# Output projection's last block by token tile for six of its eight steps, and four smaller edits at the border to the ConvFFN

## The chip, the cores and the metric

One Trainium2 chip, one of its cores. The metric is the device time of one execution in microseconds (us); the kernel before ran three times, with a median of 2329.59 us.

TensorE (PE in the profile) multiplies, VectorE (DVE) and ScalarE (ACT) work on tiles in on-chip memory and read the accumulators of TensorE, GpSimd (POOL) does what is left to it, and SyncE (SP) issues nearly all DMAs.

## The reference, cut to what matters

One layer of a diffusion backbone on 256 latent tokens of width 2048, float32. Four token mixers (a convolution, two linear-attention scans, an RWKV scan) run side by side on a normalised input; their outputs are gated, summed and projected. The change lies where that projection ends and the ConvFFN begins:

```
mx = merge_branches(...)          # sum of gated branches, then  @ w_out  (2048 x 2048)
x  = x + gt1x * rms_norm(mx, g1)
fx = conv_ffn(modulate(rms_norm(x, g2), sh2x, sc2x), ffn_up, ffn_dw, ffn_down)
x  = x + gt2x * rms_norm(fx, g3)
```

`rms_norm` is over the 2048 channels of a token, so the norm of x needs every output column of `@ w_out` for that token. `sh2x`, `sc2x`, `gt1x` and `gt2x` are slices of the adaLN product `silu(c) @ w_mod + b_mod` with w_mod 2048 x 12288.

## The kernel before, in words

**Precision and weights.** Each product is made of three matmuls on numbers split into a high and a low part: hi x hi, hi x lo, lo x hi. `load_split` (L187) brings 256 rows by 512 columns of a weight (512 KB) into a tile `raw` by a DMA on SP (L194), copies it to `hi` on ScalarE (L198) and subtracts `hi` from `raw` into `lo` (L200). The subtraction is on VectorE, but for as many calls as the counter `pool_lo` says it is on GpSimd; the counter is 0 at first and is set to 3 at L1468, ahead of the first FFN weights. `hi` and `lo` come from rings of buffers.

**The output projection** (`out_proj`, L1382). The 256 tokens are two token tiles of 128, the 2048 output columns four blocks `db` of 512. For a block, `mode_a` (L226) takes the 2048 inner rows in eight steps `kg`; a step has 6 matmuls of 128x512 for each token tile, so 96 in a block. Usually a step does both token tiles. With `apart=3`, as in the last block, the last three steps are held back and then run token tile by token tile: tile 0 for the three steps, then tile 1. The odd steps of that block use a ring of their own (`hlp`, two buffers).

After a block, for each token tile, ScalarE sums the squares of the result (L1411) and VectorE multiplies it by a gain into `mg` (L1412). After the last block `residual(i)` (L1395) follows for both tiles, one after the other, written behind the evacuation of both: the mean and a reciprocal root of the squares (`mean_rsqrt` L1373, with the seven short VectorE instructions of `rsqrt`, L104 to L115; `an`), four 512-column pieces of x + rs * mg on VectorE (L1400), their squares on ScalarE (L1402), and again mean and root (`ff`).

**The start of the FFN** (`ffn`, L1424). The second root goes on the diagonal of a matrix (`ffdiag`, L1437). `transpose_split` (L1352) multiplies x by it, for each of 16 column tiles kt, into an accumulator tile `psts` that holds both token tiles of the column; ScalarE applies shift and scale (`tst`, L1369), VectorE copies the high part (`u2h`, L1370) and subtracts it for the low part (`u2l`, L1371). Then `mode_b` (L207) runs `ffn_up` against u2: 11 pairs of blocks of eight steps, results in `psB`. Two accumulator tiles (`aux`) serve `psts` and the adaLN products.

**The adaLN product** is fed in between as a generator of steps (`mod_feed`, L296; `wmod_steps`, L248). A step loads 512 KB of w_mod (L260) and does eight matmuls into `psw`; eight steps make a block, which ends in a copy (L268), four matmuls `psf`, an addition on VectorE (L278) and a product on GpSimd (L279). `feed` (L305) takes steps until a fractional counter is reached. Ahead of the transposes L1443 takes 8 steps (`96 + 8`), after that 0.25 step for each step of `mode_b`. In the FFN `wmr` is None (L1618), so these loads use the five `raw` buffers of the FFN weights.

**What sets the order.** Each engine runs its queue in order. The queues are written before the run by the framework's planner (the kernel turns on its timeline simulation), which places instructions by their simulated readiness and, among the ready ones, in the order of the source. SP's queue is planned in the same way. A buffer that comes to lie on memory of an earlier pool waits tile by tile (`reuse_waits`) until the earlier tile has been used for the last time.

Of the kernel before, what the change touches and what calls it, by code (L numbers as in the profile page):

```python
# [11 lines left out]
F32 = mybir.dt.float32  # L12
# [8 lines left out]
P = 128  # L21
# [20 lines left out]
class Kern:  # L42
# [144 lines left out]
    def load_split(self, parts, width, rings=None):  # L187

        nc = self.nc
        raw = self.raw()  # L190
        hip, lop = rings or (self.hip, self.lop)
        for ap, o in parts:
            w = ap.shape[1]
            nc.sync.dma_start(out=raw[:, :, o : o + w], in_=ap.rearrange("(k p) c -> p k c", p=P))  # L194
        hi = hip.tile([P, 2, 512], F32R, tag="hi", name="hi")
        lo = lop.tile([P, 2, 512], F32R, tag="lo", name="lo")
        s = (slice(None), slice(None), slice(0, width))
        nc.scalar.activation(hi[s], raw[s], AF.Copy)  # L198
        self.pool_lo -= 1
        (nc.gpsimd if self.pool_lo >= 0 else nc.vector).tensor_tensor(lo[s], raw[s], hi[s].bitcast(F32), ALU.subtract)  # L200
        return hi, lo
# [24 lines left out]
    def mode_a(self, parts_of, uh, ul, nkt, toks, evac, apart=0, rings=None):  # L226

        ps = [self.mmp.tile([P, 512], F32, tag="mm", name="psA") for _ in toks]
        n2 = nkt // 2
        held = []  # L230
        for kg in range(n2):
            hl = self.load_split(parts_of(kg), 512, rings if kg % 2 else None)
            todo = [(kg, hl, ti) for ti in range(len(toks))]
            if kg >= n2 - apart:
                held.append(todo)
                todo = [t[ti] for ti in range(len(toks)) for t in held] if kg == n2 - 1 else []
            for g, (hi, lo), ti in todo:
                t0 = toks[ti]
                for k in range(2):
                    kt = 2 * g + k  # L240
                    for j, (u, w) in enumerate(((uh, hi), (uh, lo), (ul, hi))):
                        self.mm(ps[ti], u[:, kt, t0 : t0 + P], w[:, k, :],
                                start=(kt == 0 and j == 0), stop=(kt == nkt - 1 and j == 2))
            self.feed()
        evac(ps)


    def wmod_steps(self, cb, dst, raws=None, gain=None):  # L248
# [8 lines left out]
        for j in range(8):  # L257
            wr = raws or self.wmr
            raw = self.raw() if wr is None else wr.tile([P, 2, 512], F32, tag="wraw", name="wraw")
            nc.sync.dma_start(out=raw, in_=w[256 * j : 256 * j + 256, 512 * cb : 512 * cb + 512].rearrange("(k p) c -> p k c", p=P))  # L260
# [1091 lines left out]
    def transpose_split(self, src, c0, hi_of, lo_of, diag=None, mod=None):  # L1352
# [3 lines left out]
        for kt in range(KT):  # L1356
# [10 lines left out]
            else:  # L1367
                t = self.resp.tile([P, 256], F32, tag="tst", name="tst", bufs=3)
                nc.scalar.activation(t, ps[:, 0:256], AF.Identity, bias=mod[1][:, kt : kt + 1], scale=mod[0][:, kt : kt + 1])  # L1369
                nc.vector.tensor_copy(hi_of(kt), t)  # L1370
                nc.vector.tensor_tensor(lo_of(kt), t, hi_of(kt).bitcast(F32), ALU.subtract)  # L1371
# [10 lines left out]
    def out_proj(self):  # L1382
# [8 lines left out]
        wo = A["w_out"][0]  # L1391
        rings = self.hlp, self.hlp
        self.rs2 = []
# [11 lines left out]
        for db in range(4):  # L1405
            cs = slice(512 * db, 512 * db + 512)

            def ev(pss):
                for i, ps in enumerate(pss):
                    jk = self.resp.tile([P, 512], F32, tag="junk", name="junk", bufs=2)  # L1410
                    nc.scalar.activation(jk, ps, AF.Square, accum_out=ss[:, i, db : db + 1])  # L1411
                    nc.vector.tensor_tensor(mg[:, i, cs], ps, G1[:, cs], ALU.mult)  # L1412
                if db == 3:
                    residual(0)
                    residual(1)

            self.mode_a(lambda kg: [(wo[256 * kg : 256 * kg + 256, cs], 0)], self.uh, self.ul, KT, [256, 384], ev,
                        *((3, rings) if db == 3 else ()))
            if db < 2:
# [4 lines left out]
    def ffn(self):  # L1424
# [15 lines left out]
        self.fs = self.pool("ffs", bufs=2)  # L1440
        self.wap, self.rate, self.modmax = None, 0.25, 128
        self.G[1] = fp.tile([P, D], F32, name="G2")
        self.feed(96 + 8)  # L1443
        self.fed = float(self.modn)
# [22 lines left out]

        self.pool_lo = 3  # L1468
        for s in range(11):
# [75 lines left out]
    def build(self):  # L1545
# [27 lines left out]
        self.fed, self.rate, self.modn, self.modmax = 0.0, 0.0, 0, 96  # L1573
        self.pool_lo = 0
        self.mod2, self.G = self.cp.tile([P, 32, 1], F32, name="mod2"), [None, None]
# [30 lines left out]
        self.dbg("yl", self.ul[:, :, 0:256].bitcast(F32))  # L1606
        self.mgw = self.pool("mgw", bufs=3, stack=ues)
        self.mgp = self.pool("mgp", stack=ues)
        self.mg = self.mgp.tile([P, 2, D], F32, name="mg")
        self.hlp = self.pool("hlp", bufs=2, stack=ues)  # L1610
        self.resp = self.pool("resp", side="right")
# [3 lines left out]
        for i, n in enumerate((3, 0, 2, 1)):  # L1615
            self.merge(i == 0, n)
        self.out_proj()
        self.wmr = None  # L1618
        ues.close()
# [7 lines left out]
        self.hip = self.pool("hip2", bufs=4)  # L1627
        self.lop = self.pool("lop2", bufs=4)
        self.mmes = mes
        self.ffn()  # L1630
# [55 lines left out]
```

## Time and profile before

| | |
|---|---|
| three runs, us | 2334.24, 2325.4, 2329.59 (median 2329.59) |
| profiled execution, us | 2329.05 |
| its span, us | 2327.1 |
| TensorE busy | 2215.9 us, 95% of the span |
| VectorE busy | 1449.6 us, 62% |
| ScalarE busy | 989.5 us, 43% |
| GpSimd busy | 507.6 us, 22% |
| granted TensorE clock, mean | 0.977 |

A line of a timeline view gives the start, the duration, the engine, the line of the code, the operation with its output and inputs, the number of instructions, and in brackets how long the engine was idle before and what ended that. The chain view follows the work that ended last back through what released it. In a table of windows each stretch has its length, then the busy time of each engine (number of instructions), the granted TensorE clock, the DMA share and the GB/s. Times within the trace count from the start of the span.

### The profile page before, as it was taken

Reading aid. Unit: us, or ns where it says so; the run is one execution under the profiler, and the core shown is the slowest. Engines: PE = TensorE matmul, PEld = TensorE weight load, DVE = VectorE, ACT = ScalarE, POOL = GpSimd, SP = SyncE. Lnnn points to the kernel's source line nnn. Section 1 sums busy time; section 2 is a strip of 40 time slices with the busy share of each in tenths; the row PEclk is TensorE's granted clock in tenths of the full one; section 3 lists DMA queues with packets and bytes.
Section 4 is the critical chain, followed back from the end, with each engine's and each line's share of the span. In section 5 each row is a group of like instructions: output and inputs, shape, how many; then the busy total and the mean of one; then the engine's idle time right before and its main releaser. Section 6 shows DMA issues by size and latency. Waiting matters only on the chain.

```text
span 2327.1 us, 42867 instructions
## 1 busy us (share of the span) xinstructions
PE 2215.9 (95%) x16828; PEld 1812.0 (78%) x16828; DVE 1449.6 (62%) x3027; ACT 989.5 (43%) x1493; POOL 507.6 (22%) x865
## 2 busy tenths in 40 slices
PE   6979889999999989999999899989999999999998
PEld 3657667877888666777777678779999999998886
DVE  3357766734555678457565476577776677775554
ACT  4225644533554344334236434444443444444443
POOL 0012553533454599210010033010000000000000
PEclk8989999999999999999999999989999999999999
DMA  9934663555666776787777476567677666666663
GB/s 369 352 115 127 170 183 113 159 171 170 199 188 180 231 208 209 231 247 237 226 231 256 139 257 217 181 231 222 212 222 217 202 182 183 179 205 202 194 193 101
DMA packets 273867, 471.97 MB, mean 203 GB/s; under 512 B 41761, under 2 KB 80929, under 8 KB 272673
## 3 DMA queue, kind: packets, MB, share of 16 engines
q1 hardware_dynamic: 273378, 467.14, 64.8%
q8 instruction: 132, 2.16, 0.4%
q10 hardware_dynamic: 288, 2.10, 0.2%
q14 instruction: 69, 0.57, 0.1%
HBM read 440.33 MB, written 28.84 MB: 202 GB/s over the span
## 4 chain that ended last, share of the span: by engine, by line
PE 78%; DVE 8%; DMA 7%; POOL 4%; ACT 2%; issue 2%; SPq 0%; DVEq 0%; ACTq 0%; POOLq 0%
PE psB L79 37%; PE psA L79 18%; PE psD L79 10%; PE psw L79 4%; DMA wraw<-in_w_mod 3%; DVE lo L200 2%; POOL ctap L874 1%; DMA raw<-in_w_mix 1%; PE psG L79 1%; POOL cacc L875 1%; ACT hi L198 1%; PE psn L79 1%; DMA raw<-in_w_in 1%; PE psf L79 1%; DVE cacc L869 1%
## 5 line engine op out<-in xcount | busy, mean ns | idle before, releaser
L200 DVE TENSOR_TENSOR lo<-raw,hi 128x1024 fp32r<-128x1024 f32 (+2 forms) x485 | 599.2, 1236 | 458.7 <-ACT hi L198 450.0
L198 ACT ACTIVATE hi<-raw 128x1024 fp32r<-128x1024 f32 (+2 forms) x488 | 509.2, 1045 | 796.5 <-PE psB L79 348.6
L79 PE MATMUL psB<-u2h,hi 128*128 128x256 f32 x1408 | 399.5, 286 | 1.2 <-DVE u2h L1370 1.2
L79 PE MATMUL psB<-u2l,hi 128*128 128x256 f32 x1408 | 398.8, 284 | 0.5 <-DVE u2l L1371 0.5
L79 PE MATMUL psB<-u2h,lo 128*128 128x256 f32 x1408 | 399.0, 284 | 0.0
L79 PE MATMUL psA<-lo,uh 128*128 128x512 f32 x832 | 337.4, 406 | 18.4 <-DVE lo L200 18.0
L79 PE MATMUL psA<-hi,ul 128*128 128x512 f32 x832 | 332.7, 400 | 0.0
L79 PE MATMUL psA<-hi,uh 128*128 128x512 f32 x832 | 311.4, 405 | 3.2 <-DVE mg L1344 2.1
L79 PE MATMUL psB<-uh,hi 128*128 128x256 f32 (+1 forms) x832 | 281.0, 346 | 18.7 <-ACT hi L198 16.4
L79 PE MATMUL psB<-ul,hi 128*128 128x256 f32 (+2 forms) x832 | 278.5, 339 | 0.0
L79 PEld LDWEIGHTS psB<-u2h,hi 128*128 128x128 f32 x1408 | 269.6, 192 | 10.9 <-issue 9.5
L79 PEld LDWEIGHTS psB<-u2l,hi 128*128 128x128 f32 x1408 | 270.5, 192 | 0.7 <-DVE u2l L1371 0.7
L79 PE MATMUL psB<-uh,lo 128*128 128x256 f32 (+2 forms) x832 | 263.0, 339 | 8.1 <-DVE lo L200 8.1
L79 PEld LDWEIGHTS psB<-u2h,lo 128*128 128x128 f32 x1408 | 270.5, 192 | 0.1
L79 PEld LDWEIGHTS psA<-lo,uh 128*128 128x128 f32 x832 | 158.1, 190 | 68.5 <-DVE lo L200 27.5
L79 PEld LDWEIGHTS psB<-uh,hi 128*128 128x128 f32 x832 | 158.6, 191 | 51.2 <-ACT hi L198 18.5
L79 PEld LDWEIGHTS psA<-hi,uh 128*128 128x128 f32 x832 | 154.7, 190 | 53.2 <-issue 12.2
L79 PEld LDWEIGHTS psA<-hi,ul 128*128 128x128 f32 x832 | 158.3, 190 | 36.5 <-issue 2.6
L79 PEld LDWEIGHTS psB<-uh,lo 128*128 128x128 f32 (+1 forms) x832 | 152.8, 189 | 32.0 <-DVE lo L200 10.5
L79 PEld LDWEIGHTS psB<-ul,hi 128*128 128x128 f32 (+1 forms) x832 | 157.8, 190 | 23.1 <-issue 6.4
L1541 DVE TENSOR_TENSOR lo<-raw,hi 128x1024 fp32r<-128x1024 f32 x88 | 107.7, 1226 | 78.5 <-ACT hi L1540 78.5
L1461 DVE SCALAR_TENSOR_TENSOR facc<-fpad,ffdw,facc 128x256 f32<-128x256 f32 x352 | 152.8, 490 | 0.2
(573 smaller groups left out, 3028.8 us busy)
## 6 DMA issues: line engine op xcount, KB each, us to landing
raw<-in_w_in SPq DMA_DIRECT2D x208, 512.0 KB, 4.3
raw<-in_ffn_up SPq DMA_DIRECT2D x176, 512.0 KB, 3.8
wraw<-in_w_mod SPq DMA_DIRECT2D x160, 512.0 KB, 5.1
raw<-in_ffn_down SPq DMA_DIRECT2D x88, 512.0 KB, 4.5
raw<-in_w_br SPq DMA_DIRECT2D x32, 512.0 KB, 5.1
raw<-in_w_out SPq DMA_DIRECT2D x32, 512.0 KB, 4.4
raw<-in_w_mod SPq DMA_DIRECT2D x32, 512.0 KB, 3.8
raw<-in_w_in SPq DMA_DIRECT2D x48, 256.0 KB, 4.1
```

The costliest lines, as they stand in the source:

```text
L79: self.nc.tensor.matmul(out, lhsT, rhs, start=start, stop=stop)
L198: nc.scalar.activation(hi[s], raw[s], AF.Copy)
L200: (nc.gpsimd if self.pool_lo >= 0 else nc.vector).tensor_tensor(lo[s], raw[s], hi[s].bitcast(F32), ALU.subtract)
L869: nc.vector.scalar_tensor_tensor(a, cpad[:, i, t : t + 256], w(i, t), a, ALU.mult, ALU.add)
L874: nc.gpsimd.tensor_scalar(m, cpad[:, i, t : t + 256], w(i, t), None, ALU.mult)
L875: nc.gpsimd.tensor_tensor(a, a, m, ALU.add)
L1461: nc.vector.scalar_tensor_tensor(s3(acc), pad[:, dy : dy + 4, dx : dx + 64], tap(t, b), s3(acc), ALU.mult, ALU.add)
L1541: nc.vector.tensor_tensor(f(lo), f(raw), f(hi).bitcast(F32), ALU.subtract)
```

## The change

- `mode_a` of the last block holds back six steps of eight (`apart=6`), and the steps 4 to 7 use the rings of their own; these are now two pools, one for `hi` and one for `lo`, with four buffers each, opened after the merge's buffers are closed.
- `residual(i)` is called for each token tile behind that tile's own evacuation.
- GpSimd subtracts no weights any more: `pool_lo` is gone, the first three FFN weights are subtracted on VectorE like the others.
- The high part of u2 is copied by ScalarE instead of VectorE.
- The adaLN steps in the FFN load into two buffers of their own (`wmr2`); five steps instead of eight are taken ahead of the transposes, then 0.3 for each step of `mode_b`; the gain tile `G2` moves to a pool of its own.

```diff
 load_split:
         nc.scalar.activation(hi[s], raw[s], AF.Copy)
-        self.pool_lo -= 1
-        (nc.gpsimd if self.pool_lo >= 0 else nc.vector).tensor_tensor(lo[s], raw[s], hi[s].bitcast(F32), ALU.subtract)
+        nc.vector.tensor_tensor(lo[s], raw[s], hi[s].bitcast(F32), ALU.subtract)
 mode_a:
-            hl = self.load_split(parts_of(kg), 512, rings if kg % 2 else None)
+            hl = self.load_split(parts_of(kg), 512, rings if kg >= n2 - apart + 2 else None)
 wmod_steps:
-            raw = self.raw() if wr is None else wr.tile([P, 2, 512], F32, tag="wraw", name="wraw")
+            raw = wr.tile([P, 2, 512], F32, tag="wraw", name="wraw")
 transpose_split:
-                nc.vector.tensor_copy(hi_of(kt), t)
+                nc.scalar.activation(hi_of(kt), t, AF.Copy)
 out_proj:
-        rings = self.hlp, self.hlp
+        rings = self.hlp
...
-                if db == 3:
-                    residual(0)
-                    residual(1)
+                    if db == 3:
+                        residual(i)
...
-                        *((3, rings) if db == 3 else ()))
+                        *((6, rings) if db == 3 else ()))
 ffn:
-        self.wap, self.rate, self.modmax = None, 0.25, 128
-        self.G[1] = fp.tile([P, D], F32, name="G2")
-        self.feed(96 + 8)
+        self.wap, self.rate, self.modmax = None, 0.3, 128
+        self.G[1] = self.pool("ffg").tile([P, D], F32, name="G2")
+        self.feed(96 + 5)
...
-        self.pool_lo = 3
 build:
-        self.mgw = self.pool("mgw", bufs=3, stack=ues)
         self.mgp = self.pool("mgp", stack=ues)
         self.mg = self.mgp.tile([P, 2, D], F32, name="mg")
-        self.hlp = self.pool("hlp", bufs=2, stack=ues)
+        mws = ExitStack()
+        self.mgw = self.pool("mgw", bufs=3, stack=mws)
...
+        mws.close()
+        self.hlp = self.pool("hip1", bufs=4, stack=ues), self.pool("lop1", bufs=4, stack=ues)
         self.out_proj()
-        self.wmr = None
...
+        self.wmr = self.pool("wmr2", bufs=2)
```

More of the change, by code (lines that the diff above doesn't have):

```diff
@@ L1573, in build @@
         self.fed, self.rate, self.modn, self.modmax = 0.0, 0.0, 0, 96
-        self.pool_lo = 0
         self.mod2, self.G = self.cp.tile([P, 32, 1], F32, name="mod2"), [None, None]
```

## The prediction

> **What bounds the kernel now.** I read the page first, then the FFN in windows, then the chain and each engine's timeline across the border between output projection and FFN.
>
> ```profile
> 1520.00:1530.00 10.00, 5.48 (x64) 1.67 (x60) 8.87 (x37) 6.28 (x19) 1.17 (x3) 0.73 0.87 311
> 1530.00:1540.00 10.00, 7.56 (x31) 6.62 (x32) 8.73 (x17) 6.08 (x9) 7.24 (x4) 0.59 0.69 234
> 1540.00:1550.00 10.00, 8.85 (x62) 8.64 (x61) 8.01 (x16) 3.68 (x6) 1.25 (x1) 0.83 0.57 173
> 1550.00:1565.00 15.00, 15.00 (x129) 14.90 (x127) 10.88 (x21) 8.87 (x13) 0.00 (x0) 1.00 0.51 148
> ```
>
> From 1550 on TensorE is busy without a gap (15.00 of 15.00). In the thirty microseconds before it is idle for 8.1 (4.52 + 2.44 + 1.15), at a granted clock of 0.73 to 0.83. All that the change touches lies just ahead of or in this hole, so only the hole can give time; what it had absorbed, and no longer does, goes onto TensorE's path.
>
> The hole begins where the last output-projection matmul ends, T = 1495.17 + 24.78 = 1519.95 in the chain, and ends when the second column of u2 has its high part, at 1541.40 (T+21.45):
>
> ```profile
> 1495.17 24.78 PE psA L79 x106
> ```
>
> ```profile
> 1517.75 0.69 DVE L1412 TENSOR_TENSOR mg<-psA,G 128x512 f32<-128x512 f32 x1 [6.56 <-ACT junk L1411]
> ...
> 1520.07 0.16 DVE L114 TENSOR_TENSOR an0ra<-an0ra,an 128x1 f32<-128x1 f32 x1
> 1520.77 0.69 DVE L1412 TENSOR_TENSOR mg<-psA,G 128x512 f32<-128x512 f32 x1 [0.54 <-ACT junk L1411]
> ...
> 1521.63 2.74 DVE L1400 SCALAR_TENSOR_TENSOR x<-mg,an0ry,x 128x512 f32<-128x512 f32 x4
> ...
> 1526.25 1.41 DVE L1400 SCALAR_TENSOR_TENSOR x<-mg,an1ry,x 128x512 f32<-128x512 f32 x2
> 1527.58 0.15 DVE L111 SCALAR_TENSOR_TENSOR ff0ra<-ff0ra 128x1 f32<-128x1 f32 x1
> 1527.65 1.41 DVE L1400 SCALAR_TENSOR_TENSOR x<-mg,an1ry,x 128x512 f32<-128x512 f32 x2
> ...
> 1529.90 0.16 DVE L1378 TENSOR_REDUCE ff<-ss 128x1 f32<-128x4 f32 x1 [0.18 <-ACT junk L1402]
> ...
> 1531.31 2.21 DVE L112 SCALAR_TENSOR_TENSOR ff1ry<-ff1ra,ff1ry 128x1 f32<-128x1 f32 x1
> 1533.56 0.16 DVE L113 SCALAR_TENSOR_TENSOR ff1ra<-ff1ry 128x1 f32<-128x1 f32 x1
> ...
> 1534.14 0.29 DVE L1437 TENSOR_SCALAR ffdiag<-ident,ff1ry 128x128 f32<-128x128 f32 x1
> ...
> 1536.55 2.48 DVE L1371 TENSOR_TENSOR u2l<-tst,u2h 128x256 fp32r<-128x256 f32 x1
> 1538.95 2.45 DVE L1370 CAST u2h<-tst 128x256 fp32r<-128x256 f32 x1
> 1541.44 0.43 DVE L1371 TENSOR_TENSOR u2l<-tst,u2h 128x256 fp32r<-128x256 f32 x1
> 1541.78 0.29 DVE L1370 CAST u2h<-tst 128x256 fp32r<-128x256 f32 x1
> ```
>
> Two things stretch it. Token 0's evacuation comes 3.0 us ahead of token 1's, so the four x pieces of token 0 (2.74 us) run after T and ahead of token 1's. And three short VectorE instructions last 2.2 to 2.5 us each, where their neighbours take 0.16, 0.43 and 0.29: they end when GpSimd's subtractions end.
>
> ```profile
> 1531.16 2.34 POOL L200 TENSOR_TENSOR lo<-raw,hi 128x1024 fp32r<-128x1024 f32 x1 [8.48 <-ACT hi L198]
> 1535.11 1.26 POOL L279 TENSOR_TENSOR G<-G,wbg 128x512 f32<-128x512 f32 x1 [1.60 <-DVE G L278]
> 1536.33 4.93 POOL L200 TENSOR_TENSOR lo<-raw,hi 128x1024 fp32r<-128x1024 f32 x2
> ```
>
> Excess: 2.21-0.16 = 2.05, 2.48-0.43 = 2.05, 2.45-0.29 = 2.16, together 6.3 us.
>
> **The change part by part.**
>
> *The chain of token 1 alone.* With six steps held back, 36 matmuls of token 1 run behind token 0's last; 106 matmuls took 24.78 us, so these take 8.4 us. Token 0's residual is as long as that (below: about 9), so it is nearly done at T. What remains after T for token 1, from rows of either token:
> - ScalarE square and hand-over, up to the gain product: 1520.77-1519.95 = 0.82.
> - Gain product to root: token 0's went from 1517.75 to the end of L114 at 1520.23; one more short instruction (0.2): 2.68.
> - Four x pieces: 2.74.
> - Last square: 1529.90 less the end of the last x piece, 1529.06: 0.84.
> - Second root to matrix end: 1534.43-1529.90 = 4.53, less the 2.05 of the stall: 2.48.
>
> Sum 9.56, against 14.48 now: 4.9 us earlier, 2.05 of it GpSimd's stall and 2.9 token 0.
>
> *From the matrix to u2.* Now 6.97 us (1534.43 to 1541.40). After, five steps of column work in a row: psts, tst, psts, tst, hi. One of the two accumulator tiles is held by an adaLN block that stays unfinished through the transposes (5 steps of 8), so the second psts waits for the first tst to be read.
>
> ```profile
> 1534.48 0.81 PE psts L79 x2
> ...
> 1558.99 0.45 PE psts L79 x4
> ```
>
> ```profile
> 1535.32 0.56 ACT L1369 ACTIVATE tst<-psts,mod,sc 128x256 f32<-128x256 f32 x1 [2.37 <-PE psts L79]
> ```
>
> ```profile
> L1489 ACT ACTIVATE hh<-h x44: 403/421/421, 1594.2 to 2301.2; 128x256 fp32r<-128x256 f32 x44
> ```
>
> At the slow clock that is 0.85 + 0.57 + 0.85 + 0.57 + 0.42 and some hand-over, 3.4 us. The ScalarE copy is priced by the nearest one of that shape (0.42, where VectorE's took 0.29); bounds 0.29 to 0.56 (the tst row). Behind it on ScalarE stands the next tst, and VectorE's u2l waits for it instead of for VectorE. So u2's second column is there at T+12.95: 8.5 us earlier.
>
> *What the hole no longer absorbs.* From 1541.4 on TensorE still had 48 of the 64 psts records to do:
>
> ```profile
> L79 PE MATMUL psts<-ffdiag,x 128*128 128x128 f32 x48 | 8.0, 294 | 0.0
> ```
>
> ```profile
> 1555.92 2.15 PE psB L79 x18
> ...
> 1574.21 0.57 PE psw L79 x8
> ...
> 1639.45 0.87 PE psf L79 x4
> ```
>
> So four columns of four records were through, and the first column, both its parts there, had its 12 products. By T+12.95 it will be two columns and about five products. Behind: 8 records of 0.113 (0.45/4) and 7 products of 0.12 (2.15/18), 1.75 us. Three adaLN steps and the end of a block move behind the hole, at the price these have there: 3 x 0.57 + 0.87 = 2.58. Net so far 8.5 - 1.75 - 2.58 = 4.2 us.
>
> *Three subtractions come to VectorE.* 1.22 us each instead of 2.4 on GpSimd:
>
> ```profile
> L200 DVE TENSOR_TENSOR lo<-raw,hi 128x1024 fp32r<-128x1024 f32 x6 | 7.3, 1224 | 2.0 <-ACT hi L198 2.0
> ```
>
> They aren't needed before u2, but the planner puts ready work into gaps of a dependent chain: 1.41 us of x pieces stand twice in token 0's root chain (1526.25 and 1527.65 above). As the adaLN loads have left the raw ring, FFN weights will be split early, and up to four (the ring's size) can be ready at T. Bounds: none in the chain, 0; all four, 4.9. I take one in the 0.82 us wait for the square (0.4 net) and one in the chain (1.2): 1.6. Gain 2.6.
>
> *The adaLN loads.* The two own buffers are new. If their memory is free only at T, the first steps come a landing after T, the fifth two landings later; see the second rival. In the forecast the late ones are planned behind the first psts and cost 0.57 each there, 0 to 1.7 in all; I take 0. On SP a load that waits for such a buffer holds up the FFN weights behind it; five raw buffers, filled early now, cover that at nothing, without them the weights would come a landing late. The rate of 0.3 and G2's pool only move steps of 0.57 within a full TensorE: nothing.
>
> *When T comes.* Held steps eat weights at 6 matmuls, 1.4 us, each instead of 2.8; VectorE's 1.22 keeps up, and the rings of four let steps 4 to 7 be split early, but steps 2 and 3 share the old two-buffer rings: the low part of step 3 may be up to 0.8 late. Against that, at the end of the block before there is a stall today, 0.60 + 0.71, where TensorE waited for the split that came second of three:
>
> ```profile
> 1493.72 0.74 PE L79 MATMUL psA<-hi,uh 128*128 128x512 f32 x2 [0.60 <-ACT hi L198]
> 1495.17 0.51 PE L79 MATMUL psA<-lo,uh 128*128 128x512 f32 x1 [0.71 <-DVE lo L200]
> ```
>
> I put the shift of T at 0, with bounds of -1.3 and +1.3.
>
> *The clock.* It was at half again at the end of the hole:
>
> ```profile
> 1542.00:1544.00 2.00, 2.00 (x11) 0.50 0.05 19
> 1544.00:1546.00 2.00, 2.00 (x15) 0.74 0.51 110
> ```
>
> After 1541.40 this costs 2 x 0.50 + 2 x 0.26 = 1.5 us. I leave the same 1.5 behind u2's arrival; bounds for the difference -1.5 (none behind it) and 0. The Trainium skill ("TensorE: Matmul & The Clock Gate", section on what's actually happening) holds that about 3.4 us of busy time bring full rate back; a restart at T+9.6 would then leave almost none of it behind T+12.95, and the sum by that rule would be 1.2 us better (an estimate).
>
> **Sum.** 2329.05 (profiled; the median is 2329.59, so the two stand 0.5 apart) - 2.6 = **2326.4 us**.
>
> **The rivals.**
>
> *The subtractions fill the chain.* Four low parts at 1.22 ahead of the matrix: 4.2 - 4.9 leaves -0.7, 2329.8 us. For it: the two insertions above. Against: it takes all four weights loaded and copied by about T, and the first FFN weight was subtracted at 1531.16 (T+11.2).
>
> *Slower: the fifth adaLN step holds TensorE's queue.* In the source the steps stand ahead of the transposes. If the planner takes loads for fast, all five are queued ahead of psts, and the transposes wait for data.
>
> ```profile
> raw<-in_w_mod SPq DMA_DIRECT2D x11, 512.0 KB, 5.1
> ```
>
> ```profile
> SPq L260 <- PE psA L79: 5.6, 1, 5.6
> ```
>
> ```profile
> 1525.03 1.08 PE L79 MATMUL psw<-raw,cst 128*32 128x256 f32 x8 [2.79 <-DMA raw<-in_w_mod]
> ```
>
> One adaLN load already waits 5.6 us for output-projection matmuls to free its buffer, and TensorE waits 2.79 us for one. With both buffers free at T and 5.1 to land: steps end at T+6.2 and 7.3, the second pair lands at 11.3 and 12.4 and ends at 12.4 and 13.5, the fifth lands at 17.5 and ends at T+18.6. Psts at 18.6 instead of 9.56 is 9.0 later: 2329.05 - 4.2 + 9.0 = 2333.9 us. It decides from the fourth step on (13.5 gives 2328.8). The Trainium skill ("DMA: Bandwidth & Descriptors", section on the anatomy of one DMA) fits 2.0 us plus bytes over 436 GB/s to loads that GpSimd issues, 3.2 us for this load as an estimate; the fifth would then end at T+12.9 and the time be 2328.2. The row with 5.1 is the measured one.
>
> *The split by token does not happen.* If the planner lets token 1's ready matmuls pass token 0's late ones, as it does now (3.0 us of lead, where 18 matmuls would give 4.2), the 2.9 us stay: 2329.3.
>
> *ScalarE bounds the transposes.*
>
> ```profile
> L198 ACT ACTIVATE hi<-raw 128x1024 fp32r<-128x1024 f32 x10 | 10.5, 1054 | 2.2 <-PE psB L79 1.4 <-DMA raw<-in_ffn_up 0.8
> ```
>
> Two columns cost it 2 x (0.57 + 0.42) + 1.05 = 3.0 us, TensorE 24 x 0.12 + 8 x 0.113 = 3.8. If in-order waits still cost 0.2 a column, 14 give 2.8: 2329.2.
>
> **How the numbers follow.** Forecast (the chain of token 1 ends last, gain 1 to 6.7) 0.55; subtractions 0.15; late fifth step 0.18; no split 0.06; ScalarE 0.06. The forecast's own range is 2322.0 (no subtraction in the chain, 1.6; today's stall gone, 1.3; no slow clock, 1.5) to 2329. The three runs of before lie up to 4.7 from their median; about half of that for a median: 2320. High end: the slower rival's 2333.9, nearly: 2333.5. No case reaches 0.5% (11.6 us, about what a measurement of this kernel can tell from no change): the hole's idle time and slow clock hold about 10. So faster 0.06, same 0.90, slower 0.04, most of the outer two for shifts in plan or runs that I don't see.
>
> **What would show it.** Right: token 0's gain product some 8 us ahead of token 1's; no VectorE instruction of 2 us in the hole; matrix at T+9.6 to 12; u2's second column at T+13 to 16; psw between T and the matrix; no gap after. Wrong: low parts between L1378 and L1437 (first rival); TensorE idle on in_w_mod after the matrix (second); gaps of TensorE on tst; or anything that moves outside 1490 to 1560.

## The result and the profile after

The change made the kernel slower: 2344.29 us (median of five runs, 2343.53 to 2344.44) against 2325.4 us for the five runs of before beside them (2324.1 to 2334.24). The ratio is 1.0074, with a 95% interval of 1.0061 to 1.0086. The profiled execution took 2344.29 us, its span 2342.2; that is 15.1 us more than the span of before.

Each kernel has one profile, and the five runs of before lie up to 10 us apart, so what follows first compares two single executions and then asks the experiments how much of the difference is the change's.

The chain view of after, at the two places that matter (start, duration, what it was):

```profile
1507.96 16.32 PE psA L79 x70
1524.28 3.84 DMA wraw<-in_w_mod
...
1528.95 6.07 DMA wraw<-in_w_mod
...
1536.20 5.51 DMA wraw<-in_w_mod
1541.71 0.04 issue
1541.76 1.08 PE psw L79 x8
1542.84 0.73 PE psts L79 x2
...
2085.56 246.63 PE psD L79 x1051
```

The same view of before, its line for the down projection:

```profile
2076.86 240.16 PE psD L79 x1051
```

T, the end of the last output-projection matmul, moved from 1519.95 to 1507.96 + 16.32 = 1524.28: 4.3 us. From there to this piece of the down projection (the FFN's second product, accumulated in `psD`) it was 556.9 us and is 561.3: 4.4 us. The down projection has 1056 matmuls (44 steps of 24); the 1051 that the chain counts in one piece lasted 240.16 us and last 246.63: 6.5 us. Behind it nothing changed (10.1 and 10.0 us). The sum is 15.2. So the hole, the only place that the prediction argued about, holds less than a third of the loss.

The hole itself, in the windows that the prediction shows of before:

```profile
1520.00:1530.00 10.00, 5.62 (x36) 3.66 (x34) 9.28 (x20) 6.97 (x15) 0.00 (x0) 0.94 0.60 199
1530.00:1540.00 10.00, 3.46 (x26) 0.91 (x18) 8.04 (x42) 3.03 (x10) 1.16 (x3) 0.50 1.03 367
1540.00:1550.00 10.00, 7.24 (x54) 4.64 (x57) 1.28 (x3) 2.94 (x6) 0.00 (x0) 0.71 0.68 197
1550.00:1565.00 15.00, 15.00 (x131) 14.59 (x132) 6.79 (x12) 11.12 (x21) 0.00 (x0) 1.00 0.52 150
```

TensorE is idle for 4.38 + 6.54 + 2.76 = 13.7 us where it was idle for 8.1. VectorE's timeline of after shows the first reason:

```profile
1520.34 0.69 DVE L1412 TENSOR_TENSOR mg<-psA,G 128x512 f32<-128x512 f32 x1 [4.42 <-ACT junk L1411]
...
1523.06 2.74 DVE L1400 SCALAR_TENSOR_TENSOR x<-mg,an0ry,x 128x512 f32<-128x512 f32 x4
1525.71 4.63 DVE L199 TENSOR_TENSOR lo<-raw,hi 128x1024 fp32r<-128x1024 f32 x4
...
1530.32 0.68 DVE L1412 TENSOR_TENSOR mg<-psA,G 128x512 f32<-128x512 f32 x1
...
1539.21 0.28 DVE L1436 TENSOR_SCALAR ffdiag<-ident,ff1ry 128x128 f32<-128x128 f32 x1
1544.65 0.43 DVE L1371 TENSOR_TENSOR u2l<-tst,u2h 128x256 fp32r<-128x256 f32 x1 [5.16 <-ACT u2h L1370]
```

Token 0's gain product comes at T-3.9, not 8 us ahead of T; four low parts of FFN weights stand ahead of token 1's product, which comes at T+6.0. No short instruction is held for 2 us any more, that much of the change works, yet the matrix is ready at T+15.2, no earlier than before (T+14.5). From token 1's gain product to the matrix it takes 9.2 us, so the chain itself is about as short as forecast (9.56 - 0.82 = 8.7); it starts 5.2 us late. ScalarE's timeline has the other half: token 1's square, the first link of its chain, waits behind three high parts and all four squares of token 0.

```profile
1524.29 2.95 ACT L198 ACTIVATE hi<-raw 128x1024 fp32r<-128x1024 f32 x3 [3.03 <-PE psA L79]
1527.14 0.61 ACT L1402 ACTIVATE junk<-x 128x512 f32<-128x512 f32 x1
...
1529.60 0.57 ACT L1411 ACTIVATE junk<-psA 128x512 f32<-128x512 f32 x1
```

And then TensorE waits for adaLN loads (SP's timeline: the first two are issued the moment T comes, the next when a step has read its buffer):

```profile
1524.28 0.88 SPq L260 DMA_DIRECT2D wraw<-in_w_mod  x2
...
1528.95 0.38 SPq L260 DMA_DIRECT2D wraw<-in_w_mod  x1
...
1530.63 0.37 SPq L260 DMA_DIRECT2D wraw<-in_w_mod  x1
```

The fifth step ends at 1542.84, T+18.6, 3.4 us after the matrix is ready, and the second pair of transposes stands behind it: u2's first low part starts at T+20.4, where before had it at T+16.6.

### The profile page after: what moved, and what is told of

It reads as the page before. It is cut to its first block, busy times and chain, and to the rows that moved or that the text cites. A ratio compares the mean times of both kernels' runs of the same rounds, so it can differ in the third digit from the quotient of the medians.

```text
span 2342.2 us, 42861 instructions
## 1 busy us (share of the span) xinstructions
PE 2221.0 (95%) x16828; PEld 1805.5 (77%) x16828; DVE 1447.6 (62%) x3014; ACT 992.8 (42%) x1509; POOL 490.6 (21%) x862
## 4 chain that ended last, share of the span: by engine, by line
PE 78%; DVE 7%; DMA 7%; POOL 4%; ACT 3%; issue 2%; SPq 0%; DVEq 0%; ACTq 0%; POOLq 0%
PE psB L79 37%; PE psA L79 18%; PE psD L79 11%; PE psw L79 4%; DMA wraw<-in_w_mod 4%; DVE lo L199 2%; POOL ctap L874 1%; DMA raw<-in_w_mix 1%; ACT hi L198 1%; PE psG L79 1%; POOL cacc L875 1%; PE psn L79 1%; PE psf L79 1%; PE psSA L79 0%; PE psY L79 0%
## 5 line engine op out<-in xcount | busy, mean ns | idle before, releaser
L199 DVE TENSOR_TENSOR lo<-raw,hi 128x1024 fp32r<-128x1024 f32 (+2 forms) x488 | 609.7, 1251 | 459.9 <-ACT hi L198 454.4
L79 PE MATMUL psw<-wraw,cst 128*32 128x256 f32 x1536 | 129.5, 405 | 42.3 <-DMA wraw<-in_w_mod 41.9
```

Source lines behind the costliest of these rows:

```text
L79: self.nc.tensor.matmul(out, lhsT, rhs, start=start, stop=stop)
L199: nc.vector.tensor_tensor(lo[s], raw[s], hi[s].bitcast(F32), ALU.subtract)
```

## The experiments

The theory was: three separate causes. (A) The down projection's left operand, hh (the high part of its input, 128 columns to a matmul; hl is the low part), lies elsewhere: byte 172992 before, 203296 after by the layout of the pools (the traces hold no addresses), and its start address sets the pace of its matmuls. (B) The merge ahead of the output projection runs in a longer rhythm because its buffers moved. (C) In the hole the adaLN steps wait for buffers that come free only at T, and the FFN weights are split inside token 1's chain. Rivals stand with each run; the before of each ratio was run beside it, and the groups of runs were on different chips. Where a pace is given, it is the mean time from the start of one matmul to the start of the next in the trace, gaps left out.

### A: the down projection

**e1_before_operand_32.** Before, with a filler of 32 bytes ahead of hh:

```diff
         wp = self.pool("ffw", bufs=2)
+        pad = wp.tile([P, 8], F32, name="pad", bufs=1)
+        nc.vector.memset(pad, 0.0)
```

> The kernel before, with one change: a 32-byte filler tile stands ahead of the FFN's work buffers, so that the left operands of the down projection (hh, hl) start 32 bytes past a multiple of 64, as they do in the changed kernel; before, they start on a multiple of 64. Theory (start address): the down projection's matmuls go from 0.227 us each to 0.234, its 1051 recorded ones from 240 to about 246.5 us, and the kernel is 6 to 8 us slower than before. Rival (something else in the new layout or in the waits makes the changed kernel's down projection slow): no change, 0.227 and within 2 us of before.

2334.75 us (nine runs), ratio 1.0034 (1.0021 to 1.0047). The chain's line for the down projection is 5.5 us longer, at 233.4 ns a matmul where before has 226.7:

```profile
2076.94 245.64 PE psD L79 x1051
```

Thirty-two bytes in an otherwise equal program cost most of what this stage loses in after (6.5 us).

**e2_after_operand_64.** After, with the same filler, which puts hh at a multiple of 64.

> The changed kernel with the same 32-byte filler, which puts its left operands of the down projection back on a multiple of 64; nothing else is undone. Theory (start address): 0.227 us a matmul again, the kernel 6 to 8 us faster than the changed one, about 2337. Rival (the weight rings, which also lie elsewhere, or G2's pool): stays at 0.234 and about 2344.

2336.51 us (five runs), ratio 1.0044 (1.0028 to 1.0060). But the down projection ran at 232.4 ns, 244.66 us in all: 64 bytes are not the rule.

```profile
2079.01 244.66 PE psD L79 x1051
```

That the time came out as forecast, 2337, is luck: this stage gave 2.0 us, and in the profiled run T lay 6.6 us earlier than in after's, for which see B.

**f1_before_offsets.** Before, with hh and hl read at another offset every four steps.

```diff
-            hh = wp.tile([P, 256], F32R, tag="hh", name="hh", bufs=3)
+            hh = wp.tile([P, 384], F32R, tag="hh", name="hh", bufs=3)[:, o[0] : o[0] + 256]
```

> Kernel before, with the two left operands of the down projection (hh and hl) read at another offset inside their tiles every four of its 44 steps (96 matmuls a group): 0, 32, 64, 128, 192, 320, 448 bytes for both, then 32 bytes for hl alone, 32 for hh alone, 16 for both, and 0 again. Base of the tiles: 448 bytes above a multiple of 512. Theory (the start address inside 64 bytes decides): 226.7 ns from one matmul's start to the next in the groups at 0, 64, 128, 192, 320 and 448 bytes, 233 to 235 at 32 and 16, about 229 with hl alone off (a third of the products) and about 231 with hh alone. Rival (512 bytes decide): only offset 0 has 226.7. Rival (the offset is not it, the place in memory is): every group the same.

```
both at   0    32    64    128   192   320   448   16    | hl +32 | hh +32 | 0 again
ns     227.0 233.2 233.3 232.4 229.0 233.3 229.0 233.3   | 233.2  | 231.8  | 226.9
```

The first form of the theory falls: 64, 128 and 320 bytes are slow too. The second, 512 bytes, isn't refuted, since only offset 0 has 227, but 64 and 320 have one pace, and so have 192 and 448, which points to a period of 256. What fits is the distance modulo 256, counted as the start of the left operand less that of the right one: 0 gives 227, 192 (at 192 and 448) gives 229.0, 128 gives 232.4, 64 (at 64 and 320) 233.3, 32 gives 233.2. It fits for groups in which both left operands have one distance. With hl alone 32 bytes off, a third of the products, about 229 was expected and the whole group ran at 233.2; with hh alone off, 231 was expected and came (231.8). What sets the pace in a mixed stream stays open.

**f2_after_low_operand.** After, with a filler of 16 KB under the residual pool, so that hh lies at 172992 as before.

> Kernel after, with a filler of 16 KB under the residual pool, so that hh lies at byte 172992, exactly as before; weights' rings, order of the work and adaLN buffers as in after. Theory (the left operand's address alone slows the down projection): psD 240 us at 226.7 ns a matmul, 2337.5 us. Rival (the rings of the right operands, 8 KB higher than before, have a part in it, as the 232.4 ns at a multiple of 64 suggest): psD 243 to 247 us, 2340 to 2344.

2335.22 us (seven runs), ratio 1.0040 (1.0026 to 1.0055). The down projection is back at 226.7 ns:

```profile
2081.14 240.13 PE psD L79 x1051
```

The weights' rings are 8 KB higher than in before and have no part in it: 8 KB is a multiple of 256.

**g3_before_offsets_weights.** Before, with the split weights read at another offset (n times 64 bytes): they are the left operand of the FFN up projection and the right one of the down projection.

```diff
+        v = lambda t: t[:, self.off : self.off + 1024].rearrange("p (k c) -> p k c", k=2)
+        return v(hip.tile([P, 1152], ...)), v(lop.tile([P, 1152], ...))
```

> Kernel before with the split weights read at another offset in their tiles (tiles of 4608 bytes, one raw buffer less): in the FFN up projection, where they are the left operand, 192 + 64 n bytes above a multiple of 512, n from 0 to 7, another n for each of the 22 blocks in turn; in the down projection, where they are the right operand, the same for the first half of each step (four steps for each n), the left operand staying at 448. Theory A (the left operand's start in 512 bytes sets the pace, best at 448): in the up projection some n are faster or slower than the 120 ns of all blocks now, by 2 to 4 ns, best at n = 4 (448); in the down projection nothing changes. Theory B (only the distance between left and right operand counts, best at 256): up projection best at n = 4 (distance 256 to the right operand at 192); down projection best at n = 0 (226.7 ns), 229 to 235 at the others. Rival: 120 ns at all n, so only the matmuls with 512 columns are sensitive.

```
n                                  0      1      2      3      4      5      6      7
up, 256 columns, ns, lowest      119.4  113.4  118.6  115.5  119.9  113.4  118.6  115.5
of two or three blocks, highest  120.0  114.0  118.6  117.8  120.0  114.0  118.6  117.8
down, 512 columns, ns            226.9  230.3  232.6  233.3  226.7  230.3  232.6  233.3
```

The one run took 2323.91 us, and T to the first psD is 546.2 us where before has 555.5: 16 of the 22 blocks ran at 118.6 ns or less. Theory A falls: the down projection changes with the right operand's address alone. Theory B stands, with a period of 256 and not 512. It had the best place for 256 columns wrong: distance 0 is the worst there (120) and 64 the best (113.4). The kernel before has all its up projection at distance 0. It is the distance and not either address alone: modulo 256, left at 0 with right at 192 (f1, offset 64) and left at 192 with right at 128 (n = 3 here) are both 64 apart, and both give 233.3. A slow stretch also has an after-effect. The second half of each step stayed at distance 0, yet its 12 matmuls took 231.2 ns on average behind n = 1 or 5 and 228.0 to 229.3 behind 2, 3, 6 and 7, where n = 4 left them at 226.6.

**h1_before_up_distance_64, h3_after_distances.** Two fillers in u2's pool put the up projection at distance 64; h3 also has 160 bytes ahead of hh, which put the down projection of after at distance 0 without moving it out of the upper memory.

```diff
+        u2p.tile([P, 48], F32, name="gap")
         u2h, u2l = u2p.tile(...), u2p.tile(...)
+        u2p.tile([P, 16], F32, name="gap2")
```

> Kernel before with two fillers in u2's pool (192 bytes ahead of u2's high part, 64 behind its low part), so that in the FFN up projection the weights (left operand) start 64 bytes beyond the columns of u2 (right operand), counted modulo 256, instead of 0; in the down projection the distance stays 0. The order of TensorE's work is that of before. Theory (the pace follows the distance of the two operands' start addresses modulo 256): all 22 blocks of the up projection at 113.4 ns a matmul instead of 119.9, 4224 x 6.5 = 27.5 us less; the down projection at 226.7; 2300 us. Rival (the pace follows the left operand's own address, which here stays at 192): up projection at 119.9, 2327.

> Kernel after with the same two fillers in u2's pool and one of 160 bytes ahead of the FFN's small buffers, so that hh is at distance 0 from the down projection's weights (as in before) instead of 96, at byte 203456, and the up projection at 64 instead of 0. Theory (distance): up projection 113.4 ns, down projection 226.7 ns; against h1 only the hole differs, 5.2 us: 2305 to 2306 us with the same luck in the merge. Rival (the upper part of the memory is slower in itself): down projection at 230 or more, 2310.

h1: 2302.03 us (four runs, 2296.76 to 2304.86), ratio 0.9890 (0.9871 to 0.9908): 24 us less than before, from 256 bytes of filler. h3: 2308.32 us (2304.49 to 2312.12), ratio 0.9919 (0.9899 to 0.9940). The window 1900 to 2000, the up projection's matmuls alone, in before and then in h1 (all of it TensorE, at full clock):

```profile
1900.00:2000.00 100.00, 100.00 (x835) 100.00 (x834) 3.37 (x8) 3.03 (x8) 1.00 0.65 185
```

```profile
1900.00:2000.00 100.00, 100.00 (x885) 100.00 (x884) 3.77 (x9) 3.38 (x9) 1.00 0.63 195
```

835 matmuls become 885. In h1 and in h3 the up projection ran at 113.4 ns and the down projection at 226.8. The chain's line for it in h3:

```profile
2052.99 240.14 PE psD L79 x1051
```

So the upper memory is not slow in itself, and a distance of 96 was all that cost the change its 6.5 us. With the distances equal, 6.3 us are left between the medians of h3 and h1; from T to the down projection they take 534.1 and 527.4 us, 6.7 apart.

**h2_before_all_distances.** h1, and both parts of the first input at distance 0 in the stages with 512 columns.

```diff
+        ulp.tile([P, 16], F32, name="gap4")
```

> Kernel h1, and 64 bytes ahead of the low part of the first input (ul) and of the output projection's second pair of rings, so that with 512 columns both parts of the left operand start at distance 0 from the split weights instead of 0 and 192. Theory (distance): the 2496 psA matmuls at 226.7 ns instead of 230.8, 10 us less where TensorE bounds them, the psB matmuls with 256 columns and ul 118.5 to 120 (480, 1 us more); 2290 to 2294 us. Rival (psA's pace has another cause, its changes of operand): psA still at 230 to 231, 2300 as h1.

The 2496 psA matmuls went from 230.8 to 228.9 ns, half of what was expected, and the time did not move: 2302.53 us (four runs). Its trace says where the rest is. Where the stream is not interrupted by another product, as between 1450 and 1500, they run at 227.0 ns as in the down projection (230.9 in before). Elsewhere the mean is lifted by the matmuls just behind an interruption (some of 228 to 240 ns each time), and in the last block the odd steps, which read the second pair of rings, run at 233 to 234 ns, the pace of distance 64: the filler ahead of those rings missed its aim. That the time didn't follow is not explained by this alone; h2's profile has the longer merge of B, with T 3.9 us later than in h1's.

### B: the merge ahead of the output projection

**e3_before_merge_order.** Before, with the merge's pools opened in the other order, as in after.

> The kernel before, with one change: the pool of the merge's sum (mg) is opened ahead of the pool of the gate buffers, as in the changed kernel, so that the two lie the other way round. Theory (place of the gate buffers): the first gate loads start at about 1331 instead of 1303, the merge's blocks fall into the slow rhythm (6.0 us a block instead of 5.5, the second low part of a block 2.2 to 2.3 us), the merge ends 4 us later and the kernel is about 4 us slower than before. Rival (the 4 us come from elsewhere in the change or from chance): 5.5 us a block and no change.

2328.44 us (ten runs), ratio 1.0003 (0.9989 to 1.0017): the order of the pools costs nothing that these runs can tell, though the interval ends just at the 4 us of the theory. The profiled execution, one of the slowest of the ten (2333.47 us), looks as the theory forecast: gate loads at 1331.7, low parts of 2.2 to 2.3 us, T at 1527. But the link fails in other traces: e1 has its first gate load at 1303.2 and the long rhythm, f3 (next) at 1328.7 and the short one.

**f3_after_feed_96** was meant for the hole (it writes `self.feed(96)` for `self.feed(96 + 5)`) but gave the same instructions as after, one for one: on entry the counter stood at 101.75, with the rate of 0.3 at 102.05, and `feed` goes up to the larger of both. Seven steps are taken ahead of the transposes, not five. So it is after, run again.

> Kernel after with no adaLN steps queued ahead of the transposes (96 instead of 96 + 5; the rest follow at the rate of 0.3). Theory (second rival of the prediction: the queue of five steps and their landings holds up the transposes): first u2l comes 3 us earlier after the end of the output projection (T+17.5 instead of T+20.4), the loads' wait at T+20 goes too, TensorE without a gap from about T+21 instead of T+25.7; 2340 to 2341 us. Rival (VectorE's and ScalarE's chain ends last, the steps lie beside it): u2l at T+20, 2344.

2341.41 us (four runs, 2339.28 to 2348.9), ratio 1.0081 (1.0051 to 1.0111). Its profiled execution took 2339.28 us: the same program, 5.0 us faster, and with T at 1518.36 instead of 1524.28. The groups of the merge (1360 to 1410) show half of why. After:

```profile
L199 DVE TENSOR_TENSOR lo<-raw,hi 128x1024 fp32r<-128x1024 f32 x17 | 28.0, 1647 | 10.3 <-ACT hi L198 10.3
L1347 POOL TENSOR_TENSOR mg<-mg,sig 128x512 f32<-128x512 f32 x16 | 21.3, 1356 | 43.2 <-DVE sig L1346 43.2
```

The same program as f3:

```profile
L1347 POOL TENSOR_TENSOR mg<-mg,sig 128x512 f32<-128x512 f32 x18 | 29.9, 1684 | 39.5 <-DVE sig L1346 39.5
L199 DVE TENSOR_TENSOR lo<-raw,hi 128x1024 fp32r<-128x1024 f32 x18 | 24.8, 1376 | 15.6 <-ACT hi L198 15.5
```

Either VectorE's subtractions are held (mean 1647 ns) or GpSimd's additions are (1684). GpSimd's timeline gives the length of a block, from one pair of additions to the next: 6.09 us in after (they alternate between 5.97 and 6.09), 5.52 in f3.

```profile
1388.63 2.55 POOL L1347 TENSOR_TENSOR mg<-mg,sig 128x512 f32<-128x512 f32 x2 [3.42 <-DVE sig L1346]
1394.72 2.54 POOL L1347 TENSOR_TENSOR mg<-mg,sig 128x512 f32<-128x512 f32 x2 [3.54 <-DVE sig L1346]
```

```profile
1385.36 3.53 POOL L1347 TENSOR_TENSOR mg<-mg,sig 128x512 f32<-128x512 f32 x2 [2.29 <-DVE sig L1346]
1390.88 3.54 POOL L1347 TENSOR_TENSOR mg<-mg,sig 128x512 f32<-128x512 f32 x2 [1.99 <-DVE sig L1346]
```

Set side by side instruction by instruction, the two executions differ by nothing up to 790, by 3.1 us at 1324, ahead of the merge's additions, and by 5.9 at T: about half grows in the merge's blocks, the rest in small steps before.

Both rhythms occur with both orders of work: of the profiled executions with the order of before, four of seven are in the long one (additions of 1354 to 1356 ns), of those that carry the change two of ten (1356 and 1358). T is 1523.3 on average in the six long ones and 1519.4 in the eleven short ones; over all profiles it is 1521.4 with the order of before and 1520.3 with the change. So the 4.3 us ahead of T are not the change's: after's profile had the long merge and before's the short one. What decides which engine is held in a given run stays open.

### C: the hole

The measure here is the time from the end of the last psA to the first psD (the chain's piece of psD starts 1.4 us later), which neither the merge nor the pace of the down projection enters: 554.1 to 555.5 us in the kernels with the order of before (before, e1, e3, f1), 559.7 to 560.6 in those of after (after, e2, f2, f3). On average that is 5.6 us for the hole, where the one pair of profiles gave 4.4.

**e4_after_adaln_early.** After, with the two adaLN buffers in memory that comes free 5 us ahead of T.

```diff
         self.rawp = self.pool("rawp2", bufs=5)
+        self.wmr = self.pool("wmr2", bufs=2)
...
-        self.wmr = self.pool("wmr2", bufs=2)
```

> The changed kernel with the two adaLN buffers opened behind the raw ring instead of behind all weight rings; they then lie on buffers that are free 5 us before the output projection ends, instead of on uh, which is free at its end. Theory (TensorE waits for the adaLN loads): the first two steps run at once at T, the first column of u2 comes 4 to 8 us earlier after T than the 20 us of the changed kernel, and the kernel gains 4 to 8 us, about 2337 to 2340. Rival (the chain of token 1, which has its matrix at T+15.2 behind four low parts, sets the end of the hole): the matrix stays at about T+15 and the gain is under 3 us.

2340.50 us (four runs), ratio 1.0053 (1.0032 to 1.0073); T to psD 557.4 us, 2.3 less, and the matrix still at T+15.0: the rival was right. Two steps run at T without a wait, then the next pair is a landing away, as TensorE's timeline shows:

```profile
1522.83 1.07 PE L79 MATMUL psw<-wraw,cst 128*32 128x256 f32 x16
1528.35 1.08 PE L79 MATMUL psw<-wraw,cst 128*32 128x256 f32 x8 [4.45 <-DMA wraw<-in_w_mod]
```

**f4_after_all_three.** e4 and f2 together, and the edit of f3, which does nothing.

> Kernel after with three of the causes taken away at once: hh at byte 172992, the two adaLN buffers in memory that comes free early, and no adaLN steps queued ahead of the transposes. If the three add up: -6.9 - 3 to -4, so 2333 to 2334 us with the merge in its slow rhythm (blocks of 6.0 us) and 2329 with it in its fast one (5.54), which is what the kernel before takes. If the split by token then gives what was predicted: 2326 at best. If the low parts ahead of token 1's gain product bound the hole: matrix at T+15, u2l at T+17, no better than 2333 with the slow merge.

2332.79 us (ten runs), ratio 1.0022 (1.0004 to 1.0039); T to psD 557.6, as in e4. With the merge in its short rhythm, as in the profiled execution, 2329 was expected if the parts add up; that execution took 2333.04, with the matrix at T+14.8.

**g1_adaln_behind_transposes.** f2, without the call `feed(96 + 5)` (the counter stays at 96) and with the first two loads tied to u2's last column, so that no adaLN step stands ahead of the transposes.

```diff
+                nc.gpsimd.tensor_tensor(raw[:, 0, 0:1], raw[:, 0, 0:1], self.late.pop(), ALU.add)
```

> Kernel f2 (after, hh at byte 172992) with all adaLN steps of this stage put behind the transposes: none is queued ahead of them, and the first two loads are followed by a one-element addition on GpSimd that needs the last column of u2. (f3 had left the order of the work as it was: the planner's counter stood at 101.75 on entry, so 7 steps ran ahead with either number.) Theory (fifth adaLN step holds TensorE's queue): no psw between the end of the output projection T and the last transposes; matrix at T+14.8 as in f2, first u2l at T+17.4 instead of T+20.1; but 7 steps of 0.57 and 0.87 for the end of a block move onto TensorE's path, about 4.9, and 2 columns come 2.7 and 3 earlier: T to the first psD 557 to 559 us instead of 560.3, 2332 to 2334 in all. Rival (the chain on VectorE and ScalarE alone sets the hole): first u2l still at T+20, T to psD 564.

2334.73 us (nine runs), ratio 1.0029 (1.0016 to 1.0042). u2's first low part came at T+17.1 instead of T+20.1, as expected, and its second at T+17.4 instead of T+22.2, yet T to psD is 560.2, nothing gained. TensorE now idles for want of work (13.9 us in all; f2 idles 13.3 waiting for loads):

```profile
1529.56 1.20 PE L79 MATMUL psts<-ffdiag,x 128*128 128x128 f32 x4 [8.82 <-issue]
1535.61 1.22 PE L79 MATMUL psts<-ffdiag,x 128*128 128x128 f32 x4 [4.85 <-DVE ffdiag L1438]
```

What the queue of steps cost in waits it gave back in work: seven steps of 0.57 us and the end of a block are paid for behind the hole.

**g2_and_weights_behind_chain.** g1, with the split of the first four FFN weights kept behind token 1's last square (a one-element copy into the high part ahead of it).

```diff
+        if self.pin:
+            nc.scalar.activation(hi[:, 0, 0:1], self.pin.pop(), AF.Copy)
```

> Kernel g1, and the split of the first four FFN weights kept out of token 1's chain: the first high part waits for token 1's last square, the next three for the first three columns of u2 (a one-element copy on ScalarE from there into the high part ahead of it). Theory (the four low parts and three high parts ahead of token 1's square and gain product cost what they last, 4.6 us): gain product of token 1 at T+0.8 to 1.0 instead of T+5.9, matrix at T+10 to 11 (the forecast said 9.6), first u2l at T+13 to 13.7; T to psD 552.5 to 555, 2328 to 2330 us. Rival (something else is as late): matrix at T+13 or later, no gain over g1.

2333.10 us (ten runs), ratio 1.0026 (1.0015 to 1.0038); T to psD 558.2, 2.0 less than g1. Token 1's gain product came at T+2.9 (it was T+5.9), not at T+0.9, and the matrix at T+13.0, not at 10 to 11. That is the chain of 9.56 with its two known delays: the product 2.1 us late, and one low part (1.2 us) inside the second root. ScalarE's timeline (T is 1521.6) has what is late next, the last of token 0's squares, four of which still stand ahead of token 1's:

```profile
1523.12 0.63 ACT L1406 ACTIVATE junk<-x 128x512 f32<-128x512 f32 x1
1523.66 0.19 ACT L1406 ACTIVATION_READ_ACCUMULATOR junk<-x 128x1 f32 x1
1523.75 0.58 ACT L1416 ACTIVATE junk<-psA 128x512 f32<-128x512 f32 x1
```

**k1_after_hole_mended.** h3 with the early buffers of e4, four steps ahead of the transposes, and the splits of g2 kept out.

> Kernel h3 (after with the operands' distances of h1) with both causes in the hole taken away: the two adaLN buffers in memory that comes free early (as in e4), four adaLN steps ahead of the transposes and the rest behind them (as in g1), and the split of the first four FFN weights kept out of token 1's chain (as in g2). Theory (late buffers cost 2.3 to 2.5 us, e4 and f4, the splits 2.0, g2, and these add up): T to the first psD 529.5 to 530 us instead of 534.1, 2303.5 to 2304.5 us where h3 took 2308.3; no gain over h1 (527.4 and 2302). If four free steps count as well (2.3 us): 527.5 and 2301.5. Rival (the token split brings what was forecast once both are gone: 4 us better than the order of before): 523 and 2298.

2301.41 us (four runs, 2298.27 to 2309.99), ratio 0.9891 (0.9859 to 0.9923), the same as h1's 0.9890. But T to psD is 531.8 us: 2.3 less than h3, not 4.3 to 4.6, and 4.4 more than h1. The two costs do not add up, and the rival's 523 is far off. The matrix is there at T+12.9 with one low part inside the second root chain, and TensorE idles 10.7 us where h1 idles 8.3. That is 2.4 of the 4.4 us; what the other 2.0 are was not separated further. The medians can't tell k1 from h1: k1's interval reaches 7 us to either side.

## Why the prediction was wrong

**The step that failed** is the premise: "All that the change touches lies just ahead of or in this hole, so only the hole can give time". The change also moves pools, and with them operands of a stage 550 us later. The prediction asked only when memory comes free, not where it lies. It cost 6.5 us of the 15 (e1, f2 and h3: shown). It had no rival for it, and no term; "anything that moves outside 1490 to 1560" stands among its signs of being wrong, without a price. Inside the hole its sum failed as well: it forecast a gain of 2.6 us there and the hole cost 4.4 to 5.6.

**The merge.** 4.3 us of the difference between the two profiles lie ahead of T and are not the change's (f3, and T over all profiles). The prediction's forecast for the shift of T, 0 with bounds of 1.3, holds on that average (-1.1). By the ratio of all runs the change cost 17 us (14 to 20); the pace and the hole make 12 of it. The other 5 would fit if all five runs of after had the long merge; only one of them has a trace, so this is not shown.

**The lead of token 0.** The forecast took 36 matmuls, 8.4 us. ScalarE's square of token 0 ran 4.7 us ahead of T, about 20 matmuls of 0.233 us: the planner let token 1's ready matmuls pass. That is the third rival's mechanism, held at 0.06. With a lead of 4.7, token 0's squares fall behind T, where the forecast had its residual nearly done; in g2 they still hold token 1's product back by 2.1 us.

**Token 1's chain.** Forecast 9.56, plus 1.6 for low parts; measured 15.0 to 15.2. What failed is the chain's start: token 1's gain product, put at T+0.8, came at T+6.0. The first rival's price, four low parts at 1.22, was right (4.63 in the row above); its chance was too small, since the loads it asked for were in by T. The high parts on ScalarE were not in any case.

**The adaLN steps.** The second rival forecast the fifth step's end at T+18.6, from the row with 5.1 us a landing; it ended at T+18.6, and its net of 4.8 us for the whole run (2333.9 against 2329.05) is about what the hole cost (4.4). The mechanism was right; that the figures agree so closely is partly luck, since the three landings in a row took 3.84, 6.07 and 5.51 us, and since the matrix, which the rival has at T+9.56, came at T+15.2. The forecast put the late steps behind the transposes at no cost; they held the transposes 3.4 us beyond the matrix, after the 5.6 us by which the matrix itself was late. The Trainium skill ("DMA: Bandwidth & Descriptors", section on the anatomy of one DMA) would have had the fifth step end at T+12.9, an estimate from its fit for loads that GpSimd issues; these are issued by SP, and the trace sides with the measured landing. The forecast also counted five steps where there are seven, so that one step moved behind the hole and not three. As g1 shows, the queue was not a pure loss: without it TensorE idles as long (13.9 us against 13.3 in f2).

**Two readings.** The prediction gives the granted clock in the hole as 0.73 to 0.83; its own rows have 0.73, 0.59 and 0.83. No term hangs on it. It also takes 11.6 us for about the least that can be told from no change; the interval of the result, 14 to 20 us, is 6 us wide.

**What held.** No VectorE instruction is held for 2 us in the hole; ScalarE copies u2's high part in 0.42 us and bounds nothing; steady TensorE behind the hole hides the rest. What the stalls had cost was lost again to the low parts and squares that now stand in the chain, and even k1, with most of them out of it, is 4.4 us behind the old order in this stretch.

## What to carry to other kernels

A change that opens, closes or moves a pool moves operands in later stages: compare the start addresses of both operands of every matmul loop, modulo 256, before and after, and time the stages that the diff does not name. Where a dependent chain leaves an engine idle, count what fills the hole as well as what delays it; taking a delay away may only move its work behind the hole. One profile against one other can hold a difference that the same program shows against itself: profile it twice.

## What the runs showed of the hardware

The pace of a stream of 128x128 by 128x512 matmuls (fp32r, another left operand each time, full clock, no idle) depended on the distance of the two operands' start addresses (left less right) modulo 256 bytes: 226.7 ns at 0, 229 to 230 at 192, 232.5 at 128, 233.3 at 64 and 32, 234.3 at 96. With 256 columns it was 120 ns at 0, 113.4 to 114 at 64, 118.6 at 128, 115.5 to 117.8 at 192. Shifting either operand did the same (f1, g3). Streams that mix distances do not follow this table (f1 with hl alone shifted), and a change of distance slows some of the matmuls behind it (g3, h2). The Trainium skill ("TensorE: Matmul & The Clock Gate", section "Step-by-step: what each phase is for") holds that loading the next left operand takes no read bandwidth from the running matmul. A pace that hangs on the distance of the two addresses is not what one would expect from that, and the measurement decides. Whether the two reads meet in the memory, or how, no run here shows.

In the merge either VectorE's subtractions (mean 1647 ns, the others of that group 1376) or GpSimd's additions (1684 ns against 1356) were long, block after block of 6.0 to 6.1 or 5.5 us, and one program was seen in both ways (after, f3).
